# A radix-2 step in the forward transform of two long convolutions, with the complex additions on GpSimd

## The chip, the cores and the metric

The kernel runs on one core of a Trainium2 chip. The metric is the device time of one execution in microseconds (us); times of before and after are medians over several executions.

## What is computed

The reference is two layers of a hybrid backbone over 256 latent tokens of width 2048 (float32), with 256 context tokens in the first layer. Layer 0 mixes with a bidirectional state-space group and an attention group, layer 1 with an order-2 Hyena operator; a dense SwiGLU network of inner width 5632 follows each. The change lies in the Hyena operator of layer 1:

```
def long_conv_bidir(u, h_two):
    k = jnp.concatenate([h_two[:, 0], zeros, jnp.flip(h_two[1:, 1], axis=0)], axis=0)
    k = k / jnp.sum(jnp.abs(k), axis=0, keepdims=True)
    kf = jnp.fft.rfft(k, axis=0)
    uf = jnp.fft.rfft(u, n=2 * seq_len, axis=1)
    return jnp.fft.irfft(uf * kf, n=2 * seq_len, axis=1)[:, :seq_len]

proj = dwconv_centred(u @ w_in + b_in, short_w, short_b)
x1, x2, y = proj[..., :d], proj[..., d:2 * d], proj[..., 2 * d:]
for i, gate in enumerate((x1, x2)):
    y = gate * (long_conv_bidir(y, h_two) + fbias[i] * y)
return y @ w_out + b_out
```

## The kernel before

**Products in three passes.** Every product is a TensorE (PE) matmul of 128x128 weights against 256 or 512 columns. An operand is split into a rounded high half and a remainder: `split` (lines 332 to 335) takes the high half on ScalarE (ACT, line 334) and the remainder on VectorE (DVE, line 335). `mm3` (lines 362 to 369) adds three products: high with high, high with low, low with high. The large products use `wide` (lines 542 to 560), which does the first two in one matmul of 512 columns (line 556, the last one on line 559) and the third in one of 256 (line 557).

**Weights.** SP (SyncE) loads each weight tile of 1 MB in program order into a ring of raw buffers (line 339); ACT and DVE split it into `whi` and `wlo`, two halves to a tile, into a ring of three such halves. Modulation rows (`mraw`) pass through the same raw ring and are reduced on DVE (line 440).

**Layer 1.** `layer1` (line 1491) runs 48 projection tasks, six for each of eight groups `g` of 256 channels: two tasks (128 channels each) for `y`, two for the first gate, two for the second. `ev_hy` (line 1173) does one: the product of 16 blocks, the norm or bias, the short convolution on DVE (lines 1194 and 1195). When a group's `y` is there, a generator `hyena_steps(g)` (line 1216) joins a background list. After each task the list is advanced four times (`TICKS[2]`), to the generator's next `yield` each time; a scheduling layer then settles the order of instructions within each engine, so that steps of the convolutions stand between the matmuls of the tasks.

**One convolution** (here called a pair: group `g` and order `o`, 16 in all; called the first and second order below for `o` 0 and 1). `kf`, the filter's spectrum, is loaded (line 1222). Four PE transposes bring `y` to tokens on partitions (`ps_yT`, line 1228), and `split` gives `yth`, `ytl`. The forward transform is a product with a table of 256 odd frequencies, real and imaginary: for each half `f2` of the frequencies, real and imaginary part, and two halves of the tokens, one `mm3` into `ps_u` (line 1238). DVE multiplies `ps_u` with the filter (line 1243, twice), combines the products into the complex product (lines 1244 and 1245) and, with ACT, splits it into `ph`, `pl` (line 1246). After both halves, and once the gate is there, the inverse transform is eight `mm3` (two channel tiles by four parts of the spectrum) into `ps_c` (line 1258); ACT and DVE add the bias and multiply with the gate (lines 1261 to 1263). There are four yields to a pair.

The tables are split once, in `dft_steps` (line 1200), and once more at the start in `filters` (line 691), where the filter's spectrum is made and written to memory.

**After layer 1** come its output projection (`layer1_out`) and the second network, with the same weight pipeline. GpSimd (POOL) does nothing but a few memsets.

Of the kernel before, what the change touches and what calls it, by code (L numbers as in the profile page):

```python
# [10 lines left out]
F32 = mybir.dt.float32  # L11
F32R = mybir.dt.float32r
AF = mybir.ActivationFunctionType
ALU = mybir.AluOpType
# [3 lines left out]
P = 128  # L18
D = 2048
S = 256  # L20
# [82 lines left out]
def _rope_tables():  # L103
    f32 = np.float32
    n_freq = 16
    t = np.arange(S)
    inv = f32(ROPE_THETA) ** (-np.arange(n_freq, dtype=f32) / f32(n_freq))
    inv = inv.astype(f32)
    pos = np.stack([(t // GRID_W).astype(f32), (t % GRID_W).astype(f32)], axis=0)
    ang = (pos[:, None, :] * inv[None, :, None]).astype(f32)  # L110
    cos, sin = np.cos(ang), np.sin(ang)
    c64 = np.concatenate([cos[0], cos[0], cos[1], cos[1]], axis=0)
    s64 = np.concatenate([sin[0], sin[0], sin[1], sin[1]], axis=0)
    return np.concatenate([np.tile(c64, (2, 1)), np.tile(s64, (2, 1))], axis=1).astype(f32)


def _dft_angles():
    t = np.arange(S)[:, None]
    f = np.arange(256)[None, :]
    return 2.0 * np.pi * ((t * (2 * f + 1)) % 1024) / 1024.0  # L120


def _dft_forward():

    th = _dft_angles()
    m = np.concatenate([np.cos(th), -np.sin(th)], axis=1)
    return m.reshape(2, P, 512).transpose(1, 0, 2).astype(np.float32)


def _dft_inverse():  # L130
    th = _dft_angles().T
    m = np.concatenate([np.cos(th), -np.sin(th)], axis=0) / 256.0
    return m.reshape(4, P, S).transpose(1, 0, 2).astype(np.float32)


# [26 lines left out]
def _tiles(w):  # L162
    k, m = w.shape
    return w.reshape(k // P, P, m // P, P).transpose(2, 1, 0, 3).reshape(m // P, P, k)


def _prepare(inputs):
    g = {k: np.asarray(v) for k, v in inputs.items()}
    f32 = np.float32
    a = {}  # L170
# [35 lines left out]
    a["pick"] = np.tile(np.eye(32)[:, :2], (4, 1))  # L206
    a["mats"] = _const_mats()
    a["rope"] = _rope_tables()
    a["dft_f"] = _dft_forward()
    a["dft_i"] = _dft_inverse()  # L210
    embT, win = _filter_tables()
    a["embT"] = embT
# [4 lines left out]
    w = g["ev_w_in"][0]  # L217
# [17 lines left out]
    v = ukv[:, :, 128:].reshape(4, P, 4, 256).transpose(2, 1, 0, 3).reshape(4, P, 1024)  # L235
# [5 lines left out]
    for i in range(2):  # L241
        t1, t3 = _tiles(g["ffn_w1"][i]), _tiles(g["ffn_w3"][i])
# [5 lines left out]
    t = _tiles(g["hy_w_in"][0]).reshape(3, 8, 2, P, D)  # L248
# [13 lines left out]
class _Kernel:  # L262
# [428 lines left out]
    def filters(self, pool):  # L691
        nc, a = self.nc, self.a
# [3 lines left out]
        nc.sync.dma_start(embT, a["embT"])  # L696
        nc.sync.dma_start(self.mats, a["mats"])
        rawf = self.wraw.tile([P, KT * P], F32, tag="raw", name="raw_dftf")
        nc.sync.dma_start(rawf[:, :1024], a["dft_f"].rearrange("p a b -> p (a b)"))
        fh = pool.tile([P, 2, 512], F32R, name="fh0")  # L700
        fl = pool.tile([P, 2, 512], F32R, name="fl0")
        self.split(fh.rearrange("p a b -> p (a b)"), fl.rearrange("p a b -> p (a b)"), rawf[:, :1024])
# [2 lines left out]
        for j in range(3):  # L705
# [5 lines left out]
            t1 = pool.tile([P, S], F32, tag="sin1", name=self.nm("sin1"))  # L711
# [14 lines left out]
        for gi in range(8):  # L726
            g, i = gi // 2, gi % 2
# [36 lines left out]
            for f, (c0, w) in enumerate(((0, 0), (128, 0), (256, 1), (384, 1))):  # L764
                tag = ("ms", "acc")[f % 2]
# [433 lines left out]

    def dft_steps(self):  # L1200
        nc, hp = self.nc, self.hyp
        self.dfh = hp.tile([P, 2, 512], F32R, name="dfh")
        self.dfl = hp.tile([P, 2, 512], F32R, name="dfl")
        self.dih = hp.tile([P, 4, S], F32R, name="dih")
        self.dil = hp.tile([P, 4, S], F32R, name="dil")
        for k, hi, lo in (("dft_f", self.dfh, self.dfl), ("dft_i", self.dih, self.dil)):
            raw = self.wraw.tile([P, KT * P], F32, tag="raw", name=self.nm("raw_dft"))
            nc.sync.dma_start(raw[:, :1024], self.a[k].rearrange("p a b -> p (a b)"))
            yield
            for i in range(2):  # L1210
                n = hi.shape[1] // 2
                src = raw[:, i * 512:(i + 1) * 512].rearrange("p (a b) -> p a b", a=n)
                self.split(hi[:, i * n:(i + 1) * n], lo[:, i * n:(i + 1) * n], src)
                yield

    def hyena_steps(self, g):
        nc, hp = self.nc, self.hyp
        y = self.hyt[g, 0]
        for o in range(2):
            kf = hp.tile([P, 4, S], F32, tag="kf", name=self.nm("kf"), bufs=1)  # L1220
            src = self.kscr[2 * (g // 2) + o].rearrange("p (a b) -> p a b", b=512)
            nc.sync.dma_start(kf, src[:, :, (g % 2) * S:(g % 2) * S + S])
            yth = hp.tile([P, 2, S], F32R, tag="yth", name=self.nm("yth"), bufs=1)
            ytl = hp.tile([P, 2, S], F32R, tag="ytl", name=self.nm("ytl"), bufs=1)
            pst = self.ps.tile([P, 2, S], F32, tag="ms", name=self.nm("ps_yT"))
            for tt in range(2):
                for c in range(2):
                    nc.tensor.transpose(pst[:, tt, c * P:(c + 1) * P], y[:, c, tt * P:(tt + 1) * P], self.mat("ident"))
            self.split(yth, ytl, pst)
            yield from self.wait(1 + HWAITS[0])  # L1230
            ph = hp.tile([P, 4, S], F32R, tag="ph", name=self.nm("ph"), bufs=1)
            pl = hp.tile([P, 4, S], F32R, tag="pl", name=self.nm("pl"), bufs=1)
            for f2 in range(2):
                psu = self.ps.tile([P, 2, S], F32, tag=("ms", "sy")[f2], name=self.nm("ps_u"), bufs=(3, 2)[f2])
                for ri in range(2):
                    c0 = (ri * 2 + f2) * P
                    for tt in range(2):
                        self.mm3(psu[:, ri], (self.dfh[:, tt, c0:c0 + P], self.dfl[:, tt, c0:c0 + P]),
                                 (yth[:, tt], ytl[:, tt]), tt == 0, tt == 1)
                t1 = hp.tile([P, 2, S], F32, tag="t1", name=self.nm("t1"), bufs=1)  # L1240
                t2 = hp.tile([P, 2, S], F32, tag="t2", name=self.nm("t2"), bufs=1)
                for t, k in ((t1, kf[:, f2]), (t2, kf[:, 2 + f2])):
                    nc.vector.tensor_tensor(t, psu, k.unsqueeze(1).to_broadcast([P, 2, S]), ALU.mult)
                nc.vector.tensor_tensor(t1[:, 0], t1[:, 0], t2[:, 1], ALU.subtract)
                nc.vector.tensor_tensor(t1[:, 1], t1[:, 1], t2[:, 0], ALU.add)
                self.split(*[t.rearrange("p (r f) t -> p r f t", f=2)[:, :, f2] for t in (ph, pl)], t1)
                yield
            yield from self.wait(HWAITS[1])
            while (g, 1 + o, 1) not in self.hy_done:
                yield  # L1250
            if g == 0 and o == 1:
                self.mh, self.ml, self.mhl = self.pair("hmix")
            for c in range(2):
                ch = 2 * g + c
                psc = self.ps.tile([P, 512], F32, tag="ms", name=self.nm("ps_c"))
                cs = slice(c * P, (c + 1) * P)
                for f4 in range(4):
                    self.mm3(psc[:, :S], (ph[:, f4, cs], pl[:, f4, cs]), (self.dih[:, f4], self.dil[:, f4]), f4 == 0, f4 == 3)
                yc = y[:, c, :]
                t = self.small.tile([P, S], F32, tag="ft", name=self.nm("yt"), bufs=3)  # L1260
                nc.scalar.activation(t, yc, AF.Copy, scale=self.col("fbias", o * 16 + ch))
                nc.vector.scalar_tensor_tensor(t, psc[:, :S], self.kinv[:, o * 16 + ch:o * 16 + ch + 1], t, ALU.mult, ALU.add)
                nc.vector.tensor_tensor(yc, t, self.hyt[g, 1 + o][:, c, :], ALU.mult)
                if o == 1:
                    self.split(self.mh[:, ch, :S], self.ml[:, ch, :S], yc)
            yield from self.wait(1 + HWAITS[2])
        self.through.add(("hy", g))
# [292 lines left out]
```

## Time and profile before

| | |
|---|---|
| median of 3 executions | 2701.07 us (2700.0 to 2702.2) |
| the profiled execution's own time | 2700.55 us |
| its span, first to last instruction | 2698.8 us |
| mean granted TensorE clock | 0.992 |
| PE busy | 2634.9 us, 98% of the span |
| DVE busy | 2055.5 us, 76% |
| ACT busy | 1429.2 us, 53% |
| POOL busy | 0.9 us |
| layer 1, first projection matmul to last inverse matmul | 1468.7 to 1855.1 us |

The span is the profile's; the execution's own time is 1.75 us longer. A matmul's recorded duration holds its passage through the array, and the next one starts well before it ends, so what a matmul costs is read from start to start. The same holds, by less, for DVE instructions.

### The profile page before, as it was taken

To read this page: it belongs to the slowest core of one execution; us is meant where nothing else is said; L and a number is where in the kernel's file an instruction comes from. 1 tells how busy PE (TensorE), PEld (TensorE's weight loads), DVE (VectorE), ACT (ScalarE), POOL (GpSimd) and SP (SyncE) were. 2 spreads that over 40 slices of the span, in tenths; PEclk is the share of its full clock that TensorE was granted. 3 is DMA by queue.
4 is the path that set the end of the run, shared out by engine and by line. 5 is a ranking of instruction groups with operands and counts; after the bars stand their busy time and mean duration, and the time that the engine had idled before them with its cause. 6 is when DMAs were issued, how large, how long until landed. Compare 5 with 4: busy or idle time off the path is not lost.

```text
span 2698.8 us, 40059 instructions
## 1 busy us (share of the span) xinstructions
PE 2634.9 (98%) x15512; PEld 2256.6 (84%) x15512; DVE 2055.5 (76%) x3105; ACT 1429.2 (53%) x2297; POOL 0.9 (0%) x10
## 2 busy tenths in 40 slices
PE   6989999999999999999999999999999999999998
PEld 2557778988998888888889899888998888888886
DVE  6458776967798877877879999988797656656656
ACT  4463564656664544544546655545564544544545
POOL 0000000000000000000000000000000000000000
PEclk8999999999999999999999999999999999999999
DMA  8776545746578887877877655656677654655543
GB/s 332 277 256 233 200 172 205 267 153 236 201 294 297 314 301 257 323 286 256 317 272 278 225 207 203 226 198 239 214 292 272 216 187 158 216 178 181 203 159 128
DMA packets 108862, 636.15 MB, mean 236 GB/s; under 512 B 11649, under 2 KB 20225, under 8 KB 48257
## 3 DMA queue, kind: packets, MB, share of 16 engines
q1 hardware_dynamic: 104064, 625.21, 65.0%
q10 hardware_dynamic: 4608, 8.39, 0.8%
q8 instruction: 122, 2.00, 0.3%
q14 instruction: 68, 0.55, 0.1%
HBM read 623.07 MB, written 10.49 MB: 235 GB/s over the span
## 4 chain that ended last, share of the span: by engine, by line
PE 91%; DMA 3%; DVE 3%; ACT 1%; issue 1%; SPq 0%; DVEq 0%; ACTq 0%
PE acc L556 40%; PE acc L557 22%; PE acc L800 6%; PE acc L559 3%; PE acc L367 2%; PE acc L368 2%; PE acc L369 2%; DMA kscr<-ko 2%; PE ps_mod L1345 1%; DVE wlo L335 1%; PE ps_u L367 1%; PE ps_c L367 1%; DMA raw<-in_hw_in 1%; PE ps_u L368 1%; PE ps_c L368 1%
## 5 line engine op out<-in xcount | busy, mean ns | idle before, releaser
L556 PE MATMUL acc<-act,whi 128*128 128x512 f32 x3525 | 1254.9, 396 | 0.7 <-ACT whi L334 0.7
L335 DVE TENSOR_TENSOR wlo<-raw,whi 128x1024 fp32r<-128x1024 f32 (+1 forms) x842 | 938.5, 1118 | 253.4 <-ACT whi L334 249.1
L334 ACT ACTIVATE whi<-raw 128x1024 fp32r<-128x1024 f32 (+1 forms) x842 | 816.6, 973 | 480.9 <-PE acc L556 274.9
L557 PE MATMUL acc<-act,wlo 128*128 128x256 f32 x3760 | 1020.3, 282 | 3.2 <-DVE wlo L335 3.2
L556 PEld LDWEIGHTS acc<-act,whi 128*128 128x128 f32 x3525 | 665.6, 189 | 146.3 <-ACT whi L334 1.0
L557 PEld LDWEIGHTS acc<-act,wlo 128*128 128x128 f32 x3760 | 708.8, 189 | 24.5 <-DVE wlo L335 4.4
L556 PE MATMUL acc<-hh,whi 128*128 128x512 f32 x1280 | 456.5, 395 | 0.0
L440 DVE SCALAR_TENSOR_TENSOR mraw<-mraw,cb 128x2048 f32<-128x2048 f32 x160 | 365.9, 2287 | 43.2 <-DMA mraw<-in_mod 42.9
L557 PE MATMUL acc<-hh,wlo 128*128 128x256 f32 x1408 | 376.9, 282 | 0.0
L556 PEld LDWEIGHTS acc<-hh,whi 128*128 128x128 f32 x1280 | 240.9, 188 | 50.7
L557 PEld LDWEIGHTS acc<-hh,wlo 128*128 128x128 f32 x1408 | 265.2, 188 | 11.6 <-ACT hh L334 0.3
L566 ACT ACTIVATE sum<-acc 128x256 f32<-128x256 f32 x160 | 61.4, 384 | 280.8 <-PE acc L559 280.7
L368 PE MATMUL acc<-act,whi 128*128 128x258 f32 (+1 forms) x560 | 159.6, 286 | 6.4 <-DVE act L1414 6.4
L569 DVE TENSOR_TENSOR sum<-sum,acc 128x256 f32<-128x256 f32 x203 | 85.0, 419 | 103.5 <-ACT sum L566 103.3
L367 PE MATMUL acc<-act,whi 128*128 128x258 f32 (+1 forms) x560 | 160.6, 288 | 0.3 <-ACT act L1413 0.3
L369 PE MATMUL acc<-act,wlo 128*128 128x258 f32 (+1 forms) x560 | 159.0, 284 | 0.3 <-DVE wlo L335 0.3
L800 PE MATMUL acc<-act,whi 128*128 128x512 f32 x480 | 157.6, 406 | 0.0
L578 ACT ACTIVATE res<-acc,mcol 128x256 f32<-128x256 f32 x144 | 67.8, 473 | 141.2 <-PE acc L559 138.9
L581 DVE SCALAR_TENSOR_TENSOR res<-acc,mcol,res 128x256 f32<-128x256 f32 x160 | 77.0, 482 | 73.9 <-ACT res L578 63.1
L368 PEld LDWEIGHTS acc<-act,whi 128*128 128x128 f32 x560 | 107.0, 191 | 7.5 <-DVE act L1414 7.0
L369 PEld LDWEIGHTS acc<-act,wlo 128*128 128x128 f32 x560 | 107.0, 191 | 1.0 <-DVE wlo L335 1.0
L367 PEld LDWEIGHTS acc<-act,whi 128*128 128x128 f32 x560 | 107.0, 191 | 0.7 <-ACT act L1413 0.4
(322 smaller groups left out, 2892.8 us busy)
## 6 DMA issues: line engine op xcount, KB each, us to landing
raw<-in_w SPq DMA_DIRECT2D x176, 1024.0 KB, 4.9
mraw<-in_mod SPq DMA_DIRECT2D x160, 1024.0 KB, 5.1
raw<-in_w SPq DMA_DIRECT2D x128, 704.0 KB, 4.2
raw<-in_hw_in SPq DMA_DIRECT2D x48, 1024.0 KB, 4.8
raw<-in_w_in SPq DMA_DIRECT2D x29, 1024.0 KB, 5.1
mraw<-in_modn SPq DMA_DIRECT2D x16, 1024.0 KB, 8.4
mraw<-in_modn SPq DMA_DIRECT2D x32, 512.0 KB, 7.7
raw<-in_w_o SPq DMA_DIRECT2D x16, 1024.0 KB, 4.8
```

The lines of the kernel that those rows point to most:

```text
L334: nc.scalar.activation(hi, src, AF.Copy)
L335: nc.vector.tensor_tensor(lo, src, hi.bitcast(F32), ALU.subtract)
L367: t.matmul(out, lh, rh, start=first, stop=False)
L368: t.matmul(out, lh, rl, start=False, stop=False)
L369: t.matmul(out, ll, rh, start=False, stop=last)
L440: self.nc.vector.scalar_tensor_tensor(raw, raw, 1.0, self.cb, ALU.mult, ALU.mult, accum_out=self.mcol[:, j:j + 1])
L556: t.matmul(*high, start=kt == 0, stop=False, skip_group_check=True)
L557: t.matmul(ps[:, :S], wl, x[:, 0], start=False, stop=False, skip_group_check=True)
L559: t.matmul(*high, start=False, stop=True, skip_group_check=True)
L569: nc.vector.tensor_tensor(v, v, halves[0], ALU.add)
L581: nc.vector.scalar_tensor_tensor(v, halves[0], gate, v, ALU.mult, ALU.add)
L800: t.matmul(ps.rearrange("p (a b) -> p a b", a=2), w, self.act[:, j, :, kt, :S], start=kt == 0 and k == 0, stop=kt == n - 1 and k == 2)
```

## The change

The forward transform takes even and odd tokens apart. With the frequencies f (0 to 127) and 255 - f paired, the spectrum at f is E + O and, at 255 - f, the conjugate of E - O, where E and O are the products of 128 even and 128 odd tokens with one table each. So the transposes read every second token, and only half of the matmuls are needed: real and imaginary part for odd tokens, then for even tokens. ACT copies O from PSUM, DVE makes E + O and E - O, multiplies each with the filter, GpSimd makes the two additions of each complex product, and the split follows. The table of the inverse is rearranged to match, its size unchanged; the table of the forward transform is half as large; the filters keep a full-size table of their own (`dft_k`). There are six yields to a pair in place of four.

```diff
 def dft_steps(self):
-        self.dfh = hp.tile([P, 2, 512], F32R, name="dfh")
-        self.dfl = hp.tile([P, 2, 512], F32R, name="dfl")
+        self.dfh = hp.tile([P, 2, 256], F32R, name="dfh")
+        self.dfl = hp.tile([P, 2, 256], F32R, name="dfl")
...
 def hyena_steps(self, g):
...
-                    nc.tensor.transpose(pst[:, tt, c * P:(c + 1) * P], y[:, c, tt * P:(tt + 1) * P], self.mat("ident"))
+                    nc.tensor.transpose(pst[:, tt, c * P:(c + 1) * P], y[:, c, tt::2], self.mat("ident"))
...
-            for f2 in range(2):
-                psu = self.ps.tile([P, 2, S], F32, tag=("ms", "sy")[f2], name=self.nm("ps_u"), bufs=(3, 2)[f2])
+            psu = [self.ps.tile([P, 2, S], F32, tag=("ms", "sy")[tt], name=self.nm("ps_u"), bufs=(3, 2)[tt]) for tt in range(2)]
+            for tt in (1, 0):
                 for ri in range(2):
-                    c0 = (ri * 2 + f2) * P
-                    for tt in range(2):
-                        self.mm3(psu[:, ri], (self.dfh[:, tt, c0:c0 + P], self.dfl[:, tt, c0:c0 + P]),
-                                 (yth[:, tt], ytl[:, tt]), tt == 0, tt == 1)
-                t1 = hp.tile([P, 2, S], F32, tag="t1", name=self.nm("t1"), bufs=1)
-                t2 = hp.tile([P, 2, S], F32, tag="t2", name=self.nm("t2"), bufs=1)
-                for t, k in ((t1, kf[:, f2]), (t2, kf[:, 2 + f2])):
-                    nc.vector.tensor_tensor(t, psu, k.unsqueeze(1).to_broadcast([P, 2, S]), ALU.mult)
-                nc.vector.tensor_tensor(t1[:, 0], t1[:, 0], t2[:, 1], ALU.subtract)
-                nc.vector.tensor_tensor(t1[:, 1], t1[:, 1], t2[:, 0], ALU.add)
-                self.split(*[t.rearrange("p (r f) t -> p r f t", f=2)[:, :, f2] for t in (ph, pl)], t1)
+                    r = slice(ri * P, (ri + 1) * P)
+                    self.mm3(psu[tt][:, ri], (self.dfh[:, tt, r], self.dfl[:, tt, r]), (yth[:, tt], ytl[:, tt]), True, True)
+                if tt:
+                    odd = hp.tile([P, 2, S], F32, tag="odd", name=self.nm("odd"), bufs=1)
+                    nc.scalar.activation(odd, psu[1], AF.Copy)
+            ev = hp.tile([P, 2, S], F32, tag="even", name=self.nm("even"), bufs=1)
+            nc.vector.tensor_tensor(ev, psu[0], odd, ALU.add)
+            nc.vector.tensor_tensor(odd, psu[0], odd, ALU.subtract)
+            yield
+            for f2, u in enumerate((ev, odd)):
+                t = hp.tile([P, 2, S], F32, tag="t1", name=self.nm("t1"), bufs=2)
+                nc.vector.tensor_tensor(t, u, kf[:, 2 + f2].unsqueeze(1).to_broadcast([P, 2, S]), ALU.mult)
+                nc.vector.tensor_tensor(u, u, kf[:, f2].unsqueeze(1).to_broadcast([P, 2, S]), ALU.mult)
+                nc.gpsimd.tensor_tensor(u[:, 0], u[:, 0], t[:, 1], ALU.subtract)
+                nc.gpsimd.tensor_tensor(u[:, 1], u[:, 1], t[:, 0], ALU.add)
+            yield
+            for f2, u in enumerate((ev, odd)):
+                self.split(*[v.rearrange("p (r f) t -> p r f t", f=2)[:, :, f2] for v in (ph, pl)], u)
                 yield
```

**How the instructions are moved.** Three places, all in the convolution of group 2, second order; the line numbers of the changed kernel are some 13 higher. First PE, at the end of the forward transform. Before, the eleven matmuls of one frequency half (`ps_u`), with eleven more of the other half behind them:

```order
L368 MATMUL ps_u_15102<-ytl_15092,dfh 128x256
L369 MATMUL ps_u_15102<-yth_15091,dfl 128x256
L367 MATMUL ps_u_15102<-yth_15091,dfh 128x256
L368 MATMUL ps_u_15102<-ytl_15092,dfh 128x256
L369 MATMUL ps_u_15102<-yth_15091,dfl 128x256
L367 MATMUL ps_u_15102<-yth_15091,dfh 128x256
L368 MATMUL ps_u_15102<-ytl_15092,dfh 128x256
L369 MATMUL ps_u_15102<-yth_15091,dfl 128x256
L367 MATMUL ps_u_15102<-yth_15091,dfh 128x256
L368 MATMUL ps_u_15102<-ytl_15092,dfh 128x256
L369 MATMUL ps_u_15102<-yth_15091,dfl 128x256
```

Now, five for the odd tokens and five for the even ones, and then the projection's matmuls (`acc`) again:

```order
L381 MATMUL ps_u_15058<-ytl_15047,dfh 128x256
L382 MATMUL ps_u_15058<-yth_15046,dfl 128x256
L380 MATMUL ps_u_15058<-yth_15046,dfh 128x256
L381 MATMUL ps_u_15058<-ytl_15047,dfh 128x256
L382 MATMUL ps_u_15058<-yth_15046,dfl 128x256
L381 MATMUL ps_u_15057<-ytl_15047,dfh 128x256
L382 MATMUL ps_u_15057<-yth_15046,dfl 128x256
L380 MATMUL ps_u_15057<-yth_15046,dfh 128x256
L381 MATMUL ps_u_15057<-ytl_15047,dfh 128x256
L382 MATMUL ps_u_15057<-yth_15046,dfl 128x256
L570 MATMUL acc_15152<-act,wlo_14967 128x256
```

One more matmul of each `ps_u` stands a little ahead of either piece, so a pair has 24 forward matmuls before and 12 now. From the last of them to the first inverse matmul (`ps_c`), 38 projection matmuls stand here in the changed kernel. Over the 16 pairs that count is 29 to 40 in nine of them, 66 to 101 in the other seven.

Second DVE, from the first instruction that reads `ps_u`. Before, the two halves run one after the other, each with products (`t` from `ps_u` and `kf`), two additions and a split (`pl`), and with weight splits (`wlo`) between:

```order
L1243 TENSOR_TENSOR t_2603_15115<-ps_u_15102,kf_15089 128x512
L1243 TENSOR_TENSOR t_2604_15116<-ps_u_15102,kf_15089 128x512
L1194 SCALAR_TENSOR_TENSOR hyt_15156<-sum_15190,cols,hyt_15156 128x255
L1244 TENSOR_TENSOR t_2603_15115<-t_2603_15115,t_2604_15116 128x256
L1245 TENSOR_TENSOR t_2603_15115<-t_2603_15115,t_2604_15116 128x256
L335 TENSOR_TENSOR wlo_15151<-raw_15144,whi_15150 128x1024
L335 TENSOR_TENSOR pl_15101<-t_2603_15115,ph_15100 128x2x256
L1195 SCALAR_TENSOR_TENSOR hyt_15156<-sum_15190,cols,hyt_15156 128x255
L1243 TENSOR_TENSOR t_2606_15136<-ps_u_15123,kf_15089 128x512
L1243 TENSOR_TENSOR t_2607_15137<-ps_u_15123,kf_15089 128x512
L335 TENSOR_TENSOR wlo_15199<-raw_15196,whi_15198 128x1024
L1244 TENSOR_TENSOR t_2606_15136<-t_2606_15136,t_2607_15137 128x256
```

Now, sum and difference, four products in a row, then the two splits, which wait for GpSimd and ACT:

```order
L1256 TENSOR_TENSOR even_15073<-ps_u_15057,odd_15065 128x512
L582 TENSOR_TENSOR sum_15132<-sum_15132,acc_15099 128x256
L1257 TENSOR_TENSOR odd_15065<-ps_u_15057,odd_15065 128x512
L1261 TENSOR_TENSOR t_2606_15076<-even_15073,kf_15044 128x512
L1261 TENSOR_TENSOR t_2607_15081<-odd_15065,kf_15044 128x512
L1262 TENSOR_TENSOR even_15073<-even_15073,kf_15044 128x512
L1262 TENSOR_TENSOR odd_15065<-odd_15065,kf_15044 128x512
L1207 SCALAR_TENSOR_TENSOR hyt_15098<-sum_15132,cols,hyt_15098 128x255
L348 TENSOR_TENSOR wlo_15145<-raw_15142,whi_15144 128x1024
L1208 SCALAR_TENSOR_TENSOR hyt_15098<-sum_15132,cols,hyt_15098 128x255
L348 TENSOR_TENSOR pl_15056<-even_15073,ph_15055 128x2x256
L348 TENSOR_TENSOR pl_15056<-odd_15065,ph_15055 128x2x256
```

Both splits now stand behind all four products, with three other instructions ahead of them.

Third POOL, whose queue held only memsets; its first convolution:

```order
L528 MEMSET act 128x16x2 x6
L1263 ISA
L1263 TENSOR_TENSOR even_14107<-even_14107,t_2440_14110 128x256
L1264 TENSOR_TENSOR even_14107<-even_14107,t_2440_14110 128x256
L1263 TENSOR_TENSOR odd_14099<-odd_14099,t_2441_14115 128x256
L1264 TENSOR_TENSOR odd_14099<-odd_14099,t_2441_14115 128x256
```

Four additions to a pair follow in this way, 64 in all; the one `ISA` instruction ahead of the first reloads POOL's library and stands behind the memsets.

## Rows read from the trace of the kernel before

**Rows 1.** The page: busy time by engine, and the chain that ended last.
```profile
PE 2634.9 (98%) x15512; PEld 2256.6 (84%) x15512; DVE 2055.5 (76%) x3105; ACT 1429.2 (53%) x2297; POOL 0.9 (0%) x10
...
PE 91%; DMA 3%; DVE 3%; ACT 1%; issue 1%; SPq 0%; DVEq 0%; ACTq 0%
```

**Rows 2.** Windows: stretch, its length, then busy time of PE, PEld, DVE, ACT, POOL, clock, DMA.
```profile
1440.00:1500.00 60.00, 60.00 (x419) 56.06 (x418) 58.08 (x102) 43.69 (x80) 0.00 (x0) 1.00 0.72 254
1500.00:1540.00 40.00, 36.70 (x219) 31.55 (x218) 37.86 (x67) 23.26 (x41) 0.00 (x0) 1.00 0.72 249
1540.00:1860.00 320.00, 318.62 (x2040) 285.17 (x2039) 289.13 (x475) 163.52 (x254) 0.00 (x0) 1.00 0.59 211
```

**Rows 3.** Groups of PE instructions by line, 1495 to 1860 us: busy us, mean ns | idle before.
```profile
L368 PE MATMUL ps_u<-ytl,dfh 128*128 128x256 f32 x128 | 35.9, 284 | 0.0
...
L1228 PE MATMUL ps_yT<-mats,hyt 128*128 128x128 f32 x64 | 11.2, 278 | 1.0 <-DVE hyt L1263 0.9
```

**Rows 4.** Timeline of PE in a forward transform and the projection behind it: start, duration, instruction.
```profile
1543.14 0.28 PE L369 MATMUL ps_u<-yth,dfl 128*128 128x256 f32 x1
1543.26 0.28 PE L367 MATMUL ps_u<-yth,dfh 128*128 128x256 f32 x1
...
1545.54 0.28 PE L369 MATMUL ps_u<-yth,dfl 128*128 128x256 f32 x1
...
1545.78 0.40 PE L556 MATMUL acc<-act,whi 128*128 128x512 f32 x1
1546.01 0.28 PE L557 MATMUL acc<-act,wlo 128*128 128x256 f32 x1
```

**Rows 5.** Groups of DVE instructions by line and shape, 1485 to 1860 us.
```profile
L335 DVE TENSOR_TENSOR wlo<-raw,whi 128x1024 fp32r<-128x1024 f32 x95 | 115.8, 1222 | 15.2 <-ACT whi L334 14.6
...
L1243 DVE TENSOR_TENSOR t<-ps_u,kf 128x512 f32<-128x512 f32 x64 | 41.8, 684 | 6.2 <-PE ps_u L369 5.8
L335 DVE TENSOR_TENSOR pl<-t,ph 128x512 fp32r<-128x512 f32 x32 | 22.0, 686 | 1.9 <-ACT ph L334 1.6
...
L1244 DVE TENSOR_TENSOR t<-t,t 128x256 f32<-128x256 f32 x32 | 13.4, 420 | 0.2
L1245 DVE TENSOR_TENSOR t<-t,t 128x256 f32<-128x256 f32 x32 | 13.4, 419 | 0.0
```

**Rows 6.** Timeline of DVE in one frequency half of a convolution.
```profile
1619.62 1.29 DVE L1243 TENSOR_TENSOR t<-ps_u,kf 128x512 f32<-128x512 f32 x2 [1.52 <-PE ps_u L369]
1620.82 0.48 DVE L1194 SCALAR_TENSOR_TENSOR hyt<-sum,cols,hyt 128x255 f32<-128x255 f32 x1
1621.21 0.42 DVE L1244 TENSOR_TENSOR t<-t,t 128x256 f32<-128x256 f32 x1
1621.55 0.42 DVE L1245 TENSOR_TENSOR t<-t,t 128x256 f32<-128x256 f32 x1
1621.88 1.22 DVE L335 TENSOR_TENSOR wlo<-raw,whi 128x1024 fp32r<-128x1024 f32 x1
1623.02 0.69 DVE L335 TENSOR_TENSOR pl<-t,ph 128x512 fp32r<-128x512 f32 x1
1623.62 0.48 DVE L1195 SCALAR_TENSOR_TENSOR hyt<-sum,cols,hyt 128x255 f32<-128x255 f32 x1
```

**Rows 7.** Groups of ACT instructions by line and shape, 1485 to 1860 us.
```profile
L334 ACT ACTIVATE ph<-t 128x512 fp32r<-128x512 f32 x32 | 19.9, 623 | 11.6 <-DVE t L1245 11.4
...
L334 ACT ACTIVATE yth<-ps_yT 128x512 fp32r<-128x512 f32 x16 | 9.4, 589 | 10.1 <-PE ps_yT L1228 10.1
```

**Rows 8.** Groups of POOL instructions, whole span.
```profile
L515 POOL MEMSET act<- 128x32 f32 x6 | 0.7, 129 | 770.1 <-PE ps_s L369 445.4 <-PE psk L369 184.7 <-DVE wlo L335 140.0
...
L1552 POOL MEMSET const-float32-0.0<- 128x1 f32 x1 | 0.1, 98 | 0.2 <-issue 0.2
```

**Rows 9.** Timeline of POOL: its last instructions.
```profile
770.96 0.31 POOL L515 MEMSET act<- 128x32 f32 x2 [139.97 <-DVE wlo L335]
```

**Rows 10.** Waits of PE's weight loads, 1495 to 1860 us: total us, times, longest.
```profile
PEld ps_c L367 <- ACT ph L334: 2.2, 8, 0.3
```

More of the change, by code (lines that the diff above doesn't have):

```diff
@@ L114, in _rope_tables, with _dft_angles, _dft_filter @@
     return np.concatenate([np.tile(c64, (2, 1)), np.tile(s64, (2, 1))], axis=1).astype(f32)
[L117 to L120, printed above, removed]
-def _dft_forward():
-    th = _dft_angles()
-    m = np.concatenate([np.cos(th), -np.sin(th)], axis=1)
-    return m.reshape(2, P, 512).transpose(1, 0, 2).astype(np.float32)
+def _dft_angles(t, f):
+    return 2.0 * np.pi * ((t[:, None] * (2 * f[None, :] + 1)) % 1024) / 1024.0
+def _dft_filter():
+    t, f = np.arange(S), np.arange(P)
+    a, b = _dft_angles(t, f), _dft_angles(t, 255 - f)
+    m = np.concatenate([np.cos(a), np.cos(b), -np.sin(a), np.sin(b)], axis=1)
+    return m.reshape(2, P, 512).transpose(1, 0, 2).astype(np.float32)
+def _dft_forward():
+    f = np.arange(P)
+    m = []
+    for k in range(2):
+        a = _dft_angles(np.arange(k, S, 2), f)
+        m.append(np.concatenate([np.cos(a), -np.sin(a)], axis=1))
+    return np.stack(m, axis=1).astype(np.float32)
 def _dft_inverse():
-    th = _dft_angles().T
-    m = np.concatenate([np.cos(th), -np.sin(th)], axis=0) / 256.0
+    t, f = np.arange(S), np.arange(P)
+    a = _dft_angles(t, f).T
+    sign = (1 - 2 * (t % 2))[None, :]
+    m = np.concatenate([np.cos(a), sign * np.cos(a), -np.sin(a), -sign * np.sin(a)], axis=0) / 256.0
     return m.reshape(4, P, S).transpose(1, 0, 2).astype(np.float32)
@@ L208, in _prepare @@
     a["rope"] = _rope_tables()
+    a["dft_k"] = _dft_filter()
     a["dft_f"] = _dft_forward()
@@ L698, in filters @@
         rawf = self.wraw.tile([P, KT * P], F32, tag="raw", name="raw_dftf")
-        nc.sync.dma_start(rawf[:, :1024], a["dft_f"].rearrange("p a b -> p (a b)"))
+        nc.sync.dma_start(rawf[:, :1024], a["dft_k"].rearrange("p a b -> p (a b)"))
         fh = pool.tile([P, 2, 512], F32R, name="fh0")
@@ L1207, in dft_steps @@
             raw = self.wraw.tile([P, KT * P], F32, tag="raw", name=self.nm("raw_dft"))
-            nc.sync.dma_start(raw[:, :1024], self.a[k].rearrange("p a b -> p (a b)"))
+            w = hi.shape[1] * hi.shape[2] // 2
+            nc.sync.dma_start(raw[:, :2 * w], self.a[k].rearrange("p a b -> p (a b)"))
             yield
@@ L1211, in dft_steps @@
                 n = hi.shape[1] // 2
-                src = raw[:, i * 512:(i + 1) * 512].rearrange("p (a b) -> p a b", a=n)
+                src = raw[:, i * w:(i + 1) * w].rearrange("p (a b) -> p a b", a=n)
                 self.split(hi[:, i * n:(i + 1) * n], lo[:, i * n:(i + 1) * n], src)
```

## The prediction

> **What bounds the kernel now.** I start with the page. PE is busy for 98% of the span and makes 91% of the chain that ended last [rows 1], so work taken off PE can shorten the run, as far as PE is what the stretch in question waits for. That is read from the windows over layer 1 [rows 2]. From 1540 us to the layer's end at 1860 us PE is busy 318.62 of 320 us, so PE is the bound there; but DVE is busy for 289.13 us, which leaves it 30.9 us free, under 10%. From 1500 to 1540 us PE stands idle for 3.3 us while DVE is busy for 37.86 of 40: the layer's first 40 us are not PE's alone. The row from 1440 to 1500 us gives a measure of how far DVE can be loaded before it holds PE up: 58.08 of 60 us, 97%, with PE still full.
>
> Next comes what a forward matmul costs. There are three groups of 128 for `ps_u`, of which [rows 3] show one: 384 in all, at a recorded 284 ns. The timeline shows another price: from 1543.14 to 1545.54 us twenty of them start one after the other, 0.12 us apart [rows 4]. That is what one adds to a PE that is never idle. The projection's pair of matmuls costs 0.35 us in the same way (0.23 us for 512 columns, 0.12 us for 256).
>
> **The change part by part.**
>
> *Forward matmuls.* 24 to a pair become 12, so 192 go, at 0.12 us: minus 23.0 us. The first pair runs in the stretch to 1540 us, where PE waits for others anyway, so I count its 12 (1.4 us) as lost. Fifteen pairs, 21.6 us, lie in the stretch that PE bounds. That the change fails to remove them is excluded by the order, which shows the shorter piece.
>
> *Transposes with a stride.* 64 as before. They cost 11.2 us in recorded time [rows 3], so the ends are nothing and 11 us if a stride of two halves their speed. I take nothing: on DVE the split `pl`, which writes in a strided pattern, takes 0.69 us, as its plain neighbours do [rows 5].
>
> *Tables.* The forward table is half as large: two splits on ACT and DVE of half the width, some 0.35 us less each on a DVE that is full there, and a shorter load in SP's queue. I take minus 0.7 us. The filters' table is loaded and split as before, so it costs nothing.
>
> *DVE.* From start to start, a product of 512 columns takes 0.60 us (two in 1.20), an addition of 256 columns 0.335 us, a split of 512 columns 0.60 us [rows 6]. A pair loses four additions (1.34 us) and gains sum and difference (1.20 us); its four products stay. That they now read SBUF in place of PSUM changes nothing by these rows, since `pl`, which reads SBUF, has the same 0.60 us. So DVE needs 0.14 us less to a pair, 2.1 us over fifteen: 287.0 us in the stretch from 1540 us.
>
> *ACT.* One copy of 512 columns more to a pair, 0.59 us by its nearest row [rows 7], 9.4 us in all. ACT has 156 us free from 1540 to 1860 us [rows 2], and the copy runs while PE does the even tokens' matmuls. Nothing.
>
> *SP and its transfers.* The filter's load still stands between the same weight loads and still waits for DVE's last product with the old spectrum. Nothing, while DVE keeps up; if it does not, the weight loads behind it are late too.
>
> *POOL's additions.* 64 of 256 columns, and the trace has none like it. The nearest rows by engine are two memsets, 98 ns for one column and 129 ns for 32 [rows 8], 1 ns a column above some 0.1 us. Nearest by operation is DVE's addition at 0.335 us [rows 6]. An addition reads two inputs and writes one output. I take two such passes, 0.10 + 2 x 0.255 = 0.61 us, with 0.34 us as the lower end and three passes, 0.87 us, as the upper. The library's reload stands behind the last memset, at 771 us [rows 9], and has some 750 us before the first addition: nothing.
>
> *The chain from the last forward matmul to the inverse.* Before, one half's products began while PE still did the other half, and the inverse waited only 2.2 us in all [rows 10]. Now, by the order shown: sum, another instruction (0.34), difference and three products, 0.60 each, make 3.34 us to the even half's product; four POOL additions, 2.44 us; the ACT split 0.62 us [rows 7] and the DVE split 0.69 us [rows 5]: 7.1 us. PE covers this with the projection's matmuls, 29 to 40 in nine pairs (5.1 to 7.0 us, mean 6.0) and far more in the other seven. The first inverse matmuls need the even half alone, which takes off some 0.3 us. So 0.8 us is open in nine pairs, 7.2 us.
>
> *DVE and POOL beside each other.* This decides. With 21.6 us less of PE work the stretch would be 298.4 us. At the 97% that one row shows, DVE can do 289.4 us of work in it, and it has 287.0. So almost all of DVE's slack is spent by PE's own gain, and whatever POOL's 60 additions there (36.6 us) take from DVE comes back in full. The ends are none and all of it; no row of this trace has POOL reading anything, so none excludes either. I take half, 18.3 us: then DVE needs (287.0 + 18.3) / 0.97 = 314.7 us, and 16.3 us are given back. The open 7.2 us of the chain lie inside these, since PE then waits for DVE either way.
>
> The sum, against the profiled execution's own 2700.55 us: - 23.0 + 1.4 - 0.7 + 16.3 = 2694.5. The median of the executions stands 0.5 us above the profiled one, so I say **2695 us**.
>
> A rule of the Trainium skill speaks against the change. "SBUF — State Buffer", section "Who interferes with whom", says that a DVE instruction with two SBUF inputs and a GpSimd instruction that reads SBUF shut each other out for their whole length, whichever starts first. By it the sum would be the slower rival's below; no row here shows it. "GPSIMD Engine Reference", section 3.1, puts GpSimd's addition at 1.96 times DVE's, measured over 2048 columns; an estimate from it is 0.82 us for an addition, and with half taken from DVE the sum would be 2702 us.
>
> **The rivals.** *Slower: POOL's additions and DVE's instructions take turns.* The place is the queue just behind the products: products, weight splits, short convolution and `pl` all have two inputs in SBUF, and POOL starts exactly when DVE has the next of them at hand. If all 36.6 us fall on DVE, it needs 323.6 / 0.97 = 333.6 us; 35.2 us come back, and the run takes 2713.5, or **2714 us**; with additions of 0.87 us (52.2 us) 2730 us. It decides from about 30 us taken from DVE, 0.5 us to an addition: then the return is 28 us and the run is over 0.2% longer. For it: DVE issues back to back with no gap into which POOL could slip. Against it: nothing in this trace shows the two engines meeting.
>
> *Faster: they do not disturb each other.* DVE's 287 us just fit, and only the chain's open 7.2 us come back: 2700.55 - 23.0 + 1.4 - 0.7 + 7.2 = 2685.5, **2686 us**; 2679 us if that is covered too. For it: DVE runs at 97% in another stretch while PE stays full. Against it: DVE is so near its limit that any wait in its queue reaches the weight splits behind.
>
> **How the numbers follow.** I give the half-way case 0.50, with a range of its own from 2687 to 2704 us (additions of 0.34 to 0.87 us), the slower rival 0.30 and the faster one 0.20. About 0.2% (5.4 us) is what a measurement of this kernel can tell from no change, so faster means under 2695.7 us and slower over 2706.5. The half-way case lies around the lower bound: 0.24 faster, 0.24 same, 0.02 slower. Together: faster 0.44, same 0.24, slower 0.32. The range goes from 2679, the faster rival with its chain covered, to 2720, the slower rival at some 0.7 us to an addition; the 2730 of its upper price stays out.
>
> **What would show it.** Right: 192 forward matmuls in the profile, PE's idle time in layer 1 up by some 15 us and ended by `wlo` or `ph`, DVE busy 97% there, `wlo` splits longer than 1.22 us where a POOL addition runs. Taking turns would show as such longer DVE instructions summing to over 30 us, or as POOL additions drawn out. No disturbance would show as unchanged DVE means and a layer 1 some 15 to 22 us shorter. POOL additions well over 0.9 us, or a change outside layer 1, would make the whole account wrong.

## The result, and the profile after

The changed kernel takes **2729.5 us** (median; 2725.9 to 2733.1), beside 2700.5 us of the kernel before on the same chip: a ratio of 1.0103, with a 95% interval from 1.0090 to 1.0116. It is 29 us slower, outside the forecast range.

Nothing outside layer 1 explains this. The two profiled executions, 2725.9 and 2700.55 us, are 25.4 us apart. In them the last inverse matmul starts at 1879.1 and at 1855.1 us, so 24 of the 25.4 us are lost by the end of layer 1. The windows over the layer, in the order of columns of [rows 2], are these of the changed kernel (the layer itself now ends at 1879 us; a short window stands behind the long ones):

```profile
1500.00:1540.00 40.00, 34.72 (x200) 29.99 (x199) 38.18 (x66) 26.33 (x46) 4.12 (x4) 0.96 0.65 226
1540.00:1860.00 320.00, 291.93 (x1735) 255.40 (x1734) 283.48 (x412) 157.18 (x245) 66.56 (x56) 0.97 0.55 197
...
1760.00:1780.00 20.00, 16.72 (x85) 14.36 (x85) 14.55 (x23) 9.49 (x16) 0.00 (x0) 0.83 0.50 190
```

PE is busy for 291.93 of 320 us, where it was busy for 318.62 [rows 2]. DVE is *not* full: 283.48 us, 89%. So both engines have time left, and what is missing is in the waits between them. The waits of PE's weight loads in the changed kernel, 1495 to 1890 us (total us, times, longest), name the chain; before, the first of them was 2.2 us [rows 10]:

```profile
PEld ps_c L380 <- ACT ph L347: 23.1, 15, 3.0
PEld ps_yT L1242 <- DVE hyt L1284: 10.2, 5, 3.6
PEld acc L570 <- DVE wlo L348: 7.9, 8, 2.0
PEld ps_c L382 <- DVE pl L348: 3.1, 7, 1.2
PEld acc L569 <- ACT whi L347: 2.4, 3, 2.0
```

These are 46.7 us; PE's matmuls, which the loads run ahead of, stand idle for 35.4 us of them. The second row is the second order of a group: its transposes wait for the first order's result, a wait that the prediction has no term for. And `ph`, for which PE waits most, waits itself for POOL. The groups of POOL, ACT and DVE in the changed kernel over the same stretch (busy us, mean ns | idle before) answer to [rows 5, 7]:

```profile
L1263 POOL TENSOR_TENSOR even<-even,t 128x256 f32<-128x256 f32 x16 | 21.3, 1328 | 1033.5 <-DMA raw<-in_hw_in 757.4 <-DVE even L1262 193.6 <-ACT yt L1282 82.5
L1264 POOL TENSOR_TENSOR odd<-odd,t 128x256 f32<-128x256 f32 x16 | 16.0, 1000 | 0.0
...
L347 ACT ACTIVATE ph<-even 128x512 fp32r<-128x512 f32 x16 | 10.1, 630 | 34.4 <-POOL even L1264 34.4
...
L348 DVE TENSOR_TENSOR wlo<-raw,whi 128x1024 fp32r<-128x1024 f32 x97 | 127.2, 1317 | 14.2 <-ACT whi L347 9.2 <-PE acc L570 4.9
L1208 DVE SCALAR_TENSOR_TENSOR hyt<-sum,cols,hyt 128x255 f32<-128x255 f32 x43 | 22.8, 531 | 0.0
L348 DVE TENSOR_TENSOR pl<-even,ph 128x512 fp32r<-128x512 f32 x16 | 19.3, 1207 | 11.1 <-ACT ph L347 11.1
L1261 DVE TENSOR_TENSOR t<-even,kf 128x512 f32<-128x512 f32 x16 | 10.9, 680 | 0.0
```

`pl` of the even half has gone from 686 ns [rows 5] to 1207, `wlo` from 1222 to 1317. The even half's products, which run before POOL starts, are as they were (680 ns). One pair shows why; this is the timeline of POOL and then DVE in the changed kernel (start, duration, instruction):

```profile
1677.13 1.06 POOL L1263 TENSOR_TENSOR even<-even,t 128x256 f32<-128x256 f32 x1 [23.68 <-ACT yt L1282]
1678.14 0.91 POOL L1264 TENSOR_TENSOR even<-even,t 128x256 f32<-128x256 f32 x1
1679.01 1.72 POOL L1263 TENSOR_TENSOR odd<-odd,t 128x256 f32<-128x256 f32 x1
1680.69 1.18 POOL L1264 TENSOR_TENSOR odd<-odd,t 128x256 f32<-128x256 f32 x1
```
```profile
1677.50 0.96 DVE L1208 SCALAR_TENSOR_TENSOR hyt<-sum,cols,hyt 128x255 f32<-128x255 f32 x1
1678.39 1.74 DVE L348 TENSOR_TENSOR wlo<-raw,whi 128x1024 fp32r<-128x1024 f32 x1
1680.05 1.22 DVE L348 TENSOR_TENSOR pl<-even,ph 128x512 fp32r<-128x512 f32 x1
1681.20 1.75 DVE L348 TENSOR_TENSOR wlo<-raw,whi 128x1024 fp32r<-128x1024 f32 x1
```

Each DVE instruction is about half a microsecond longer than alone (0.48, 1.22, 0.68 and 1.22 us), and each POOL addition is longer than the 0.72 us that the shortest of them takes; the longest, 1.72 us, lies beside a `wlo` of 1.74 us. The four additions take 4.74 us, from 1677.13 to 1681.87. Behind the first two, which complete the even half, comes its `ph`, for which PE has stood idle 1.29 us when the inverse starts.

### The profile page after: what moved, and what is told of

Its sections match the earlier page's. It is cut to its first block, busy times and chain, and to the rows that moved or that the text cites. A ratio compares the mean times of both kernels' runs of the same rounds, so it can differ in the third digit from the quotient of the medians.

```text
span 2724.1 us, 39766 instructions
## 1 busy us (share of the span) xinstructions
PE 2627.5 (96%) x15320; PEld 2244.6 (82%) x15320; DVE 2071.9 (76%) x3073; ACT 1437.8 (53%) x2313; POOL 75.7 (3%) x74
## 4 chain that ended last, share of the span: by engine, by line
PE 85%; DVE 7%; DMA 3%; ACT 2%; issue 2%; POOL 1%; SPq 0%; POOLq 0%; DVEq 0%; ACTq 0%
PE acc L569 37%; PE acc L570 20%; PE acc L813 6%; PE acc L572 3%; PE acc L380 3%; PE acc L381 3%; PE acc L382 3%; DVE wlo L348 2%; PE ps_mod L1366 1%; DMA kscr<-ko 1%; ACT whi L347 1%; DMA raw<-in_hw_in 1%; DVE mraw L453 1%; PE ps_y L1058 1%; PE ps_o L1180 1%
```

## The experiments

Theories for the first four: **A**, POOL's additions and DVE's instructions take turns, which draws both out and lengthens the chain PE waits for; **B**, the radix-2 form itself leaves PE without cover; **C**, POOL is only slow and disturbs nobody.

**The additions back on DVE.**

```
-                nc.gpsimd.tensor_tensor(u[:, 0], u[:, 0], t[:, 1], ALU.subtract)
-                nc.gpsimd.tensor_tensor(u[:, 1], u[:, 1], t[:, 0], ALU.add)
+                nc.vector.tensor_tensor(u[:, 0], u[:, 0], t[:, 1], ALU.subtract)
+                nc.vector.tensor_tensor(u[:, 1], u[:, 1], t[:, 0], ALU.add)
```

> The radix-2 step as changed, with the complex additions on DVE. Theory A (POOL's additions and DVE's instructions with two SBUF inputs take turns, which draws both out and lengthens the chain that PE waits for): most of the 29 us goes away; DVE gets 60 x 0.335 = 20 us more in the stretch, so it becomes the bound and the time is 2690 to 2703 us. Theory B (the radix-2 form itself, one long chain of sum, difference and four products, leaves PE without cover, whoever adds): still 2715 us or more, with PE's waits for ph near 40 us. Theory C (POOL is only slow, 0.72 us against 0.335, without disturbing DVE): some 1.5 us less in 13 pairs, 2705 to 2712 us.

Measured: 2699.8 us, ratio to the kernel before 0.9987 (0.9977 to 0.9996), in A's range and outside the others'. The loss is gone, so it came with POOL and B falls. But of the 23 us of forward matmuls nearly nothing is left, and the windows of this kernel say where it went:

```profile
1540.00:1860.00 320.00, 309.07 (x1909) 273.90 (x1908) 309.30 (x519) 174.84 (x272) 0.00 (x0) 0.99 0.61 220
```

DVE is busy for 309.30 of 320 us, 97%. That its load is what PE now waits for is tested below, by moving some of it away.

**POOL alone, on the old transform.** Lines 1244 and 1245 of the kernel before on `nc.gpsimd`, nothing else.

> The kernel before, with only its complex additions moved to GpSimd; the forward transform keeps its 24 matmuls to a pair. Theory A: slower than before by 8 to 30 us, POOL's additions at 1.0 us or more on average and DVE's weight splits longer than 1.22 us. Theory B: within 5 us of before, since the long chain is absent. Theory C: 0 to 8 us slower, additions at 0.72 us, DVE's means unchanged.

Measured: 2737.5 us, ratio 1.0127 (1.0108 to 1.0145). The 64 additions cost 36 us without any radix-2 step, more than the 8 to 30 us of A and far from the ranges of B and C. Their means are 1119 and 1110 ns, and PE waits 21.9 us for `ph`.

**Additions that nobody waits for, and memsets in their place.** In the kernel before, behind the gate of each pair:

```
+            m, gate = self.mats, self.hyt[g, 1 + o]
+            for i in range(4):
+                c0 = (4 + 2 * (i % 2)) * P
+                nc.gpsimd.tensor_tensor(m[:, c0:c0 + S], gate[:, i // 2, :], m[:, 8 * P:10 * P], ALU.add)
```

and in the second kernel one addition of 8 columns in front, and in the loop `nc.gpsimd.memset(m[:, 4 * P:9 * P], 0.0)`.

> The kernel before, with 64 more additions of 256 columns on GpSimd, four to a pair, that start when a gate is there and whose result nobody reads (they add to a spare part of the constants). Nothing waits for them, so any cost is disturbance. Theory A: additions drawn out from 0.72 to 1.0 us or more, weight splits on DVE longer than 1.26 us on average, DVE's instructions of layer 1 together 20 to 45 us longer, the time 0 to 12 us above before as DVE had 31 us free. Theories B and C: additions at 0.72 us, DVE's means as before, the time as before.

> The same place, but GpSimd does four memsets of 640 columns to a pair (and one addition of 8 columns, which ties them to the gate): as long on POOL as an addition, but reading nothing. If the turns of theory A come from the reading of SBUF, DVE's weight splits stay at 1.22 us and the time is that of before within 3 us; if POOL's writes disturb DVE too, weight splits get longer as in the run with additions.

Measured: idle additions 2709.9 us, ratio 1.0026 (1.0016 to 1.0036); idle memsets 2700.4 us, ratio 0.9997 (0.9987 to 1.0006). The same two DVE groups, first with the additions, then with the memsets:

```profile
L335 DVE TENSOR_TENSOR wlo<-raw,whi 128x1024 fp32r<-128x1024 f32 x105 | 132.3, 1266 | 10.2 <-ACT whi L334 9.9
L440 DVE SCALAR_TENSOR_TENSOR mraw<-mraw,cb 128x2048 f32<-128x2048 f32 x20 | 46.9, 2343 | 1.5 <-DMA mraw<-in_mod 1.5
```
```profile
L335 DVE TENSOR_TENSOR wlo<-raw,whi 128x1024 fp32r<-128x1024 f32 x108 | 131.4, 1221 | 16.6 <-ACT whi L334 16.1
L440 DVE SCALAR_TENSOR_TENSOR mraw<-mraw,cb 128x2048 f32<-128x2048 f32 x20 | 45.7, 2285 | 1.4 <-DMA mraw<-in_mod 1.3
```

POOL is busy in both (68.2 and 46.4 us from 1540 to 1860 us). DVE becomes longer where POOL reads 256 columns at a time, not where it writes; C falls. The time (8 us above before), the additions (1190 ns in the mean) and `wlo` are as A expected; the sum on DVE is not, since its busy time from 1540 to 1860 us rises by 7.4 us only (289.13 to 296.54) in place of 20 to 45 over the layer. The second kernel's POOL instructions (minimum, median, maximum ns) show the other side:

```profile
L1254 POOL MEMSET mats<- x64: 631/634/639, 1512.2 to 1843.8; 128x640 f32 x64
L1252 POOL TENSOR_TENSOR mats<-hyt,mats x16: 201/212/2092, 1512.0 to 1839.5; 128x8 f32<-128x8 f32 x16
```

A memset varies by 8 ns; an addition of only 8 columns takes 0.20 us or, drawn out, up to 2.09.

**Half of the additions, and DVE given room.** The next four go together. The first leaves `add` on GpSimd and puts `subtract` on VectorE. The others change two numbers of the table of rates, which moves 17 of the 20 modulation rows out of the layer into the feed-forward network ahead of it (with the additions on VectorE; in the kernel before; in the changed kernel):

```
-MODS = (1.8, 0.6, 0.55, 0.4, 0.6)
+MODS = (1.8, 0.6, 0.70, 0.0, 0.6)
```

> The changed kernel with the subtraction of each complex product on VectorE and only its addition on GpSimd: 32 GpSimd additions in place of 64. Theory A (a GpSimd addition and the VectorE instructions that read two SBUF operands take turns, which draws both out and lengthens the chain that TensorE waits for): less than the changed kernel's loss but some of it, 2703 to 2718 us; the 32 additions still take over 1.0 us in the mean, and TensorE's wait for the rounded inverse operand lies between that of the changed kernel (23.1 us) and that with all additions on VectorE (7.3 us). Theory B (any trip to GpSimd and back costs a fixed handover in the chain, however many additions lie in it): one trip is left per half, so 2715 us or more. Theory C (only the number of VectorE instructions decides): 2695 to 2706 us.

> The form with the complex additions on VectorE, and the modulation rows that it took in layer 1 (about 19 instructions of 2.28 us on VectorE, 43 us) moved forward into the first feed-forward network, where TensorE is busy all of the time and VectorE 80%: only two numbers of the table of rates differ (0.55 to 0.70 and 0.4 to 0). Theory D (with the additions on VectorE the radix-2 step's saving on TensorE is held back because VectorE is the bound of layer 1, 97% busy): 2682 to 2692 us, VectorE at some 85% between 1540 and 1860 us and TensorE's waits there under half of what they were. Theory E (the chain of one pair is too long for the cover that TensorE has left, whatever VectorE's load): 2695 to 2702 us, with the waits unchanged.

> The kernel before with the same two numbers moved (modulation rows out of layer 1 into the first feed-forward network). Both theories: TensorE is the bound of layer 1 in this kernel, so 2696 to 2704 us, no change that can be measured, or a few us faster by the waits that are left. If it gains 10 us or more, the rows themselves held layer 1 up and a gain of the other kernel with moved rows is not the radix-2 step's.

> The changed kernel (additions on GpSimd) with the same two numbers moved. Theory A (turns between GpSimd's additions and VectorE's instructions lengthen the chain): the modulation rows are the longest VectorE instructions with two SBUF operands, so without them a part of the loss goes, but the splits of the weights stay and the additions still take about 1 us: 2700 to 2720 us, and slower than the form with the additions on VectorE and the same rows moved by 10 us or more. Theory D' (VectorE's load alone makes the loss): it falls to that form's time, 2682 to 2692 us.

Measured: half of the additions 2705.2 us, ratio 1.0016 (1.0004 to 1.0028): in the range of A, and B's fixed price for the trip is out. It lies in C's range too (2695 to 2706 us); but with 32 instructions fewer on DVE this kernel is slower than the one with all additions there, so their number alone does not decide. PE waits 8.5 us for `ph`, hardly more than without POOL (7.3), so the loss of 5.4 us against all additions on VectorE lies elsewhere: PE waits 12.8 us for `pl` and `wlo` together, against 7.9. A VectorE subtraction of the even half, 0.41 us when nothing is beside it, has a median of 0.96 us here. The other three make a table with what was there:

| | rows in layer 1 | rows moved | moving them |
|---|---|---|---|
| kernel before | 2701.6 | 2698.1 | -3 |
| radix-2, additions on VectorE | 2699.8 | **2674.0** | -26 |
| radix-2, additions on GpSimd (the change) | 2729.5 | 2703.5 | -26 |

(2701.6 is the median of 25 executions of the kernel before, beside those of the right column.) With intervals against the kernel before, the right column is 0.9986 (0.9976 to 0.9995), 0.9900 (0.9881 to 0.9920) and 1.0010 (1.0000 to 1.0019). Three things follow. Once DVE has room, the radix-2 step is worth 2698.1 - 2674.0 = 24 us: theory D, and more of it than was expected (2682 to 2692 us); E falls. GpSimd's additions cost 29.7 us in one column and 29.4 in the other, whether DVE is short of time or not, so that price is no matter of DVE's total load and D' falls (2703.5 us is in A's range). And the kernel before gains only 3 us, so the rows alone held nothing up there. The last row says one thing more: the rows on DVE cost the changed kernel 26 us too, although DVE is at 89% in it and not at 97%. The two prices add. (The rows take their transfers with them, the DMA share of the stretch falling from 0.61 to 0.52 with the additions on DVE; that DVE's instructions are what counts is likely from the 97%, not shown apart.) The waits and the window of the fast kernel (radix-2, additions on VectorE, rows moved):

```profile
1540.00:1860.00 320.00, 318.15 (x1973) 282.90 (x1973) 292.43 (x499) 182.97 (x285) 0.00 (x0) 1.00 0.52 181
```
```profile
PEld ps_u L380 <- ACT yth L347: 2.3, 9, 0.3
PEld acc L570 <- DVE wlo L348: 1.1, 3, 0.6
...
PEld ps_c L380 <- ACT ph L347: 0.6, 3, 0.2
```

DVE is at 91% (not the 85% expected, since the layer is shorter and the next network's work moves up into the window), PE is full again, and the last inverse matmul starts at 1822.9 us.

**Where the 29 us lie.** The fast kernel again, with idle additions at the place of the change's own (what they write is read by nobody):

```
                 nc.vector.tensor_tensor(u, u, kf[:, f2].unsqueeze(1).to_broadcast([P, 2, S]), ALU.mult)
+                for j in range(2):
+                    c0 = (4 + 2 * j) * P
+                    nc.gpsimd.tensor_tensor(self.mats[:, c0:c0 + S], t[:, j], self.mats[:, 8 * P:10 * P], ALU.add)
```

and beside it the half-way kernel with the rows moved.

> The form with the additions on VectorE and the modulation rows moved (2674 us), with 64 more GpSimd additions of 256 columns at the place where the changed kernel has its own, reading the same product tile and a spare part of the constants, and nobody waits for what they write. It splits the 29 us that GpSimd's additions cost in two. Theory F (most of it is that VectorE's instructions are drawn out while GpSimd reads, whoever waits for GpSimd): 2688 to 2703 us. Theory G (most of it is that GpSimd's four additions, 1.0 to 1.5 us each, lie in the chain that TensorE waits for; the drawing out of others costs what the idle additions cost in the kernel before, some 8 us): 2676 to 2687 us, with few waits of TensorE for the rounded inverse operand.

> The changed kernel with the subtractions on VectorE, the additions on GpSimd, and the modulation rows moved. Theory A: 32 additions with 1.0 to 1.4 us each, each beside a VectorE subtraction of 0.42 us that does the other half of the product, still lengthen the chain and draw VectorE's work out, and VectorE has no lack of time any more that they could relieve: 2677 to 2690 us, slower than with all on VectorE (2674). Rival: with half of them GpSimd takes work off VectorE at no cost: 2666 to 2674 us.

Measured: the idle additions 2702.3 us, ratio 1.0006 (0.9997 to 1.0015), that is 28 us above the fast kernel, without one instruction that waits for POOL's results. F's range holds and G's does not: what the additions do to DVE can by itself cost as much as the 29 us. The half-way kernel 2689.8 us, ratio 0.9956 (0.9943 to 0.9968), is at the upper end of A's range: 16 us slower than with none on GpSimd, so even half of them take off nothing. DVE's instructions on the even half, in the kernel with idle additions (minimum, median, maximum ns):

```profile
L1261 DVE TENSOR_TENSOR t<-even,kf x16: 675/680/682, 1524.5 to 1843.7; 128x512 f32<-128x512 f32 x16
L1262 DVE TENSOR_TENSOR even<-even,kf x16: 682/1228/1234, 1525.7 to 1844.9; 128x512 f32<-128x512 f32 x16
L1266 DVE TENSOR_TENSOR even<-even,t x16: 412/952/962, 1528.0 to 1847.2; 128x256 f32<-128x256 f32 x16
L1267 DVE TENSOR_TENSOR even<-even,t x16: 412/952/961, 1528.8 to 1848.0; 128x256 f32<-128x256 f32 x16
```

At either length, an instruction that an addition draws out is 0.54 us longer: 0.68 becomes 1.23, 0.41 becomes 0.95. In the mean over the 16 pairs the even half's second product gains 0.51 us (1.20 against 0.68), the odd half's 0.30 (0.99 against 0.68), the even half's two sums 0.39 and 0.44: 1.64 us to a pair, 26 us in all, and all of it in the chain that ends in `ph` and `pl`. PE's waits for these two rise from 0.9 to 23.7 us. Those of the earlier run, beside other instructions, cost 8 us. So the price depends on whom an addition meets.

What this run does not show is that the change's own 29 us come about in the same way. Its idle additions lie beside the chain's own sums, which the change does not have on DVE, and beside the even half's second product, which in the change is done before POOL starts. The waits differ too. First the fast kernel with idle additions, then the change with the rows moved:

```profile
PEld ps_c L380 <- ACT ph L347: 14.3, 11, 2.3
PEld ps_c L382 <- DVE pl L348: 9.4, 9, 1.9
PEld ps_u L380 <- ACT yth L347: 2.5, 9, 0.3
```
```profile
PEld ps_c L380 <- ACT ph L347: 11.5, 7, 2.4
PEld ps_u L380 <- ACT yth L347: 9.8, 12, 1.6
PEld ps_c L382 <- DVE pl L348: 7.2, 15, 0.6
...
ACT ph L347 <- POOL even L1264: 37.3, 16, 3.3
ACT ph L347 <- POOL odd L1264: 15.2, 15, 2.2
```

In the change the additions themselves stand in the chain, and ACT waits 52.5 us for them. How much of the 29 us is their undisturbed length (0.72 us against the 0.335 of DVE's from start to start), how much the drawing out of them and of DVE's instructions, no run separates.

## Why the prediction was wrong

- *Forward matmuls, minus 23.0 us.* Right. With DVE given room, the step as a whole brings 24.0 us, beside 23.7 for matmuls and tables together. The 1.4 us that I counted as lost in the first pair aren't lost there: PE is busy for 39.9 us from 1500 to 1540 us in that kernel, where DVE has room.
- *Transposes with a stride.* 305 ns recorded in place of 278 [rows 3], 64 times: under 2 us in recorded time, and 282 ns with the same stride where the additions are on DVE. Nothing, as taken. *ACT's copy*: nothing, as taken.
- *POOL's additions, 0.61 us.* Mis-sized: 0.72 us at the least, 1.0 to 1.3 in the mean. The fixed part is larger than the memset suggested: 0.20 us for 8 columns, in place of 0.10 for one.
- *The chain, 7.1 us against a cover of 6.0.* Four additions were to take 2.44 us of it; in the pair shown they take 4.74. The inverse starts behind the even half's two alone, 1.92 us, for which I had taken off 0.3 us; even so PE waits there.
- *DVE and POOL beside each other.* **This is the step that failed**: "then DVE needs (287.0 + 18.3) / 0.97 = 314.7 us, and 16.3 us are given back. The open 7.2 us of the chain lie inside these". I priced the meeting of the two engines as throughput that DVE lacks, took half, and let the chain vanish in it. Beside the 22.3 us that matmuls and tables were to win, a loss of 29.0 us means that 51 us were given back, not 16.3. The runs show two prices that add. The first is the load on DVE, and it needs no POOL: with the additions on DVE some 20 us are given back (2699.8 us where the matmuls and tables alone make 2678), and moving other work off DVE regains them, in the changed kernel too, where DVE is at 89%. The second is POOL's, 29.4 and 29.7 us, and room on DVE does not lower it. An addition and a DVE instruction that meet can both become longer; in the pair shown they meet in the chain from the last forward matmul to the inverse, and PE waits for its end.
- *The slower rival* had the mechanism, with a chance of 0.30, and its upper price, 2730 us, is what was measured; but it reached that number by DVE's throughput at 97% too, so that the agreement of the sum is luck in good part. The 2730 was left out of the range because I held 0.87 us an unlikely price; in turns an addition takes more than that.
- *Its bound on DVE*, 97%, holds for another kernel: with the additions on VectorE, DVE is at 97% and takes back nearly all of the 23 us.
- *The rule of the Trainium skill.* "SBUF — State Buffer", section "Who interferes with whom", says that a DVE instruction with two SBUF inputs and a GpSimd instruction that reads SBUF exclude each other. The trace agrees in what matters: the pairs that it names became longer (`wlo`, `pl`, `hyt`, the products and sums), POOL's memsets disturbed nobody, and in the pair shown 2.9 us of additions (4 x 0.72) and 3.3 us of DVE work (start to start, undisturbed: 0.39 + 1.15 + 0.60 + 1.15) took 5.7 us from 1677.13 to 1682.87, almost their sum of 6.2. "For their whole length", as I put it in the prediction, is not what is measured: a DVE instruction that is drawn out loses 0.54 us, less than the 0.72 of an addition alone. I gave the rule less weight than it deserved, since no row had shown it. My estimate of 0.82 us, from the 1.96 of the Trainium skill, "GPSIMD Engine Reference", section 3.1, misses the 0.72 of an undisturbed addition by as much as my 0.61 does.
- *What I said would show it.* Taking turns was to appear as drawn-out additions, and did, with 1.20 us in the mean of all 64; that is also the sign, well over 0.9 us, that was to make the whole account wrong. Its other sign, longer DVE instructions summing to over 30 us, did not appear: the sum is some 22 us. PE's idle time from 1540 to 1860 us rose by 27 us in place of 15. DVE at 97% did not appear.
- *A slip in a sum.* The upper end of the half-way case, 2704 us, comes out as 2703 by its own terms; nothing hangs on it.

A part of the loss went through the clock. The granted clock stood at 0.97 over the long window and at 0.83 from 1760 to 1780 us, at 1.00 before [rows 2]. Taken microsecond by microsecond from 1495 to 1900 us, it falls six times in the changed kernel to 0.50, the lower of its two levels (1.2 in place of 2.4 GHz). Each time it falls during a wait of PE (1.7 to 3.3 us) or right behind it, and is back at 1.00 after PE has been at work again. One of them, the 3.28 us wait for `hyt` that ends at 1764.18 us:

```profile
1762.00:1763.00 1.00, 0.00 (x0) 0.00 (x0) 1.00 (x4) 0.35 (x1) 0.00 (x0) 1.00 0.68 279
...
1766.00:1767.00 1.00, 1.00 (x4) 0.84 (x4) 1.00 (x1) 1.00 (x1) 0.00 (x0) 0.50 0.00 0
...
1770.00:1771.00 1.00, 1.00 (x8) 0.87 (x7) 0.00 (x0) 0.22 (x1) 0.00 (x0) 1.00 1.03 434
```

An estimate from these windows, the missing part of the clock summed up, is 12 us in the changed kernel, 3.4 with the rows moved, 1.7 in the fast kernel with idle additions and nothing in the fast kernel and the kernel before. So of the 29.4 us with the rows moved the clock has 3.4 at most. It comes with the waits; no run took the waits without it.

## What to carry to other kernels

Before an engine's work is moved to GpSimd, look at what the other engine runs in that moment, and at whether a third one waits for both: the price is in the chain, so a share of busy time under 90% is no comfort, and work that nobody waits for can cost as much as work in the chain (28 us here). Where a saving on the bound engine leaves the next engine at 97%, make room there first, by moving instructions whose place in time is free. Here that, and no GpSimd, made the version that beats both: **2674.0 us**, 1.0% below the kernel before.

## What the runs showed of the hardware

- A DVE instruction with two SBUF inputs that a GpSimd addition of 128 x 256 draws out is 0.54 us longer, less than the 0.72 us that the addition takes alone and the same for DVE instructions of 0.41 and 0.68 us.
- The addition itself can lose more than that. Beside DVE instructions issued back to back it took up to 2.79 us in the changed kernel, and one of the idle ones 5.94. From its start, at 1579.55 us, nine DVE instructions in a row ran at their undisturbed lengths; only the tenth was longer:

```profile
L1263 POOL TENSOR_TENSOR even<-even,t x16: 848/1056/2786, 1524.9 to 1871.7; 128x256 f32<-128x256 f32 x16
```
```profile
L1265 POOL TENSOR_TENSOR mats<-t,mats x64: 728/1091/5941, 1525.2 to 1847.8; 128x256 f32<-128x256 f32 x64
```

- DVE instructions that read PSUM beside their SBUF input were not longer in the same stretches: `sum<-sum,acc` has a mean of 410 ns in the changed kernel, 409 with the idle additions in the fast kernel and 413 in that one without POOL. In the change with the rows moved eleven of them lie beside an addition, each at 0.41 us.
